# Three terms of a list scheduler's cost model changed: matmul time, a shared VectorE/GpSimd port, DRAM load latency

## The chip, the cores and the metric

The kernel runs on one core of a Trainium2 chip. The metric is the device time in microseconds of one execution. Engines are called PE (TensorE, with PEld for its weight loads), DVE (VectorE), ACT (ScalarE), POOL (GpSimd) and SP (SyncE, which issues all DMAs here).

## The reference

One layer of a hybrid encoder trunk, over 2048 rows of width 1024, all in float32. One projection `u = x @ w_in` feeds three groups of heads. Their outputs, each gated by a SiLU path, are concatenated, projected again and normalised:

```python
u = x @ w_in
(fq, fk, fv, ff, fz, mq, mk, mv, mi, mf, mo, mz, rq, rz) = jnp.split(u, split_points, axis=-1)
y_fox = forgetting_attention(fq, fk, fv, ff + fox_f_bias) * jax.nn.silu(fz)      # 6 heads x 64, causal
qk = jax.nn.silu(causal_depthwise_conv(jnp.concatenate([mq, mk], axis=-1), conv_w, conv_b))
mq_c, mk_c = jnp.split(qk, [MLSTM_WIDTH], axis=-1)
y_ml = mlstm(mq_c, mk_c, mv, mi + i_bias, mf + f_bias, mo, norm_g) * jax.nn.silu(mz)   # 4 heads x 96
mem_k, mem_v = jnp.split(mem @ w_mem_kv, [MEM_WIDTH], axis=-1)
y_mem = memory_attention(rq, mem_k, mem_v) * jax.nn.silu(rz)                     # 4 heads x 64, 256 tokens
y = jnp.concatenate([y_fox, y_ml, y_mem], axis=-1) @ w_out
return layer_norm(DEEPNORM_ALPHA * x + y, ln_g, ln_b)
```

## The kernel before

**Arithmetic.** Float32 products are made from a high and a low part of each operand in the fp32r format: three matmuls (high*high, low*high, high*low) in place of one. The parts of a loaded tile `raw` are `h` (written by ACT) and `l` (written by DVE). Attention weights come out of ACT as `ph` (high) and `p` (full), DVE makes `pl = p - ph`, and POOL sums `acc = acc + p` for the denominators.

**Tiling.** The sequence is cut into four blocks of 512 rows and two halves of two blocks each. `PROJ` lists the projection jobs: 128 columns of one head's q and k (`h`), values and gates (`v`), mLSTM rows (`r`, 288 columns) and columns (`c`), memory queries (`rq`), gates. Each job is a run of matmuls into a PSUM tile `pj`. A finished job starts the work that hangs on it.

**Attention items.** One head over one block of queries is an item; there are 40, numbered from 0 in the order in which they are added. Items 0 to 7 and 20 to 27 are memory attention (2 chunks of 128 keys each), 8 to 19 the first half of the causal heads (4 or 8 chunks), 28 to 39 the second half (12 and 16 chunks in turn). An item runs through `att_max` (maxima, tile `mx`), `att_qk` and `att_exp` (for every chunk: two matmuls into `st`, two exponentials on ACT, the subtraction `pl` on DVE, the sum `acc` on POOL), `att_pv` (for every chunk: `o<-ph,v`, then `o<-pl,v`) and `att_end`. There are two buffers for `st`, two for `p` (and one for `acc`), two for `ph` and three for `pl`, the last two with the buffers `ta` to fall back on. Items 28 to 39 run as six pairs, each pair one head's two blocks, 28 chunks.

**mLSTM and output.** When the loader has reached the output weights `wo`, `ml_unit` tiles (16 of 128 rows, two in flight) load `mq`, `mk`, `vv` and `dd` from scratch DRAM, update the state `cst` and write to `y_scr`. `out_tile` (16 tiles) reads `y_scr` as `yr`, splits it into `yh` and `ylo`, and multiplies by `wo`. The 32 buffers of the tag `x`, which hold the parts of the input, take the parts of `wo` as the last projections give them up.

**What sets the order.** Nothing of the order is written by hand beyond `PROJ`. Every piece above is a generator that yields instructions. `Machine.run` simulates the five engines while the program is built: at each step it takes the engine whose next ready instruction could start earliest by the model, and on that engine the thread of highest priority (`PRIO`: loads first, then ends and maxima, `pv`, `qk`, mLSTM, projections, output). `Op.__init__` gives an instruction's cost in ns, `Machine.when` the time at which its inputs are there (with 200 ns between engines), and `Machine.issue` advances the clocks and emits it. The order so found is the program's order on each engine; on the chip each engine runs its instructions in that order and waits on semaphores. All instructions are emitted in `issue`, so all carry one line in the profile, L204 (L212 in the changed kernel); groups are told apart by tile names.

Of the kernel before, what the change touches and what calls it, by code (L numbers as in the profile page):

```python
# [14 lines left out]
BF16 = mybir.dt.bfloat16  # L15
# [4 lines left out]
DRAM = bass.MemoryType.DRAM  # L20
# [56 lines left out]
class Op:  # L77


    def __init__(self, eng, fn, args, kw):  # L80
        self.eng, self.fn, self.args, self.kw = eng, fn, args, kw
        ap = [a for a in args if hasattr(a, "tensor")]
        out = kw.get("out", ap[0] if ap else None)
        ins = ap[1:] if "out" not in kw else ap
        ins = ins + [v for k, v in kw.items() if k != "out" and hasattr(v, "tensor")]
        self.out = out.tensor.name
        self.ins = [a.tensor.name for a in ins]
        size = lambda a: math.prod(a.shape[1:])
        cols = size(out)
        wide = max([cols] + [size(a) for a in ins])  # L90
        if eng == "PE":
            f32 = ins[0].dtype == F32
            if f32 and fn.__name__ != "transpose":
                self.cost = 2.0 * max(2.0 * cols / 2.4, 107.0)
            else:
                self.cost = max((2.0 if f32 else 1.0) * cols / 2.4, 53.0 if ins[0].dtype == BF16 else 107.0)
        elif eng == "ACT":
            self.cost = 70.0 + 0.835 * wide + 115.0 * sum(hasattr(kw.get(a), "tensor") for a in ("bias", "scale"))
        elif eng == "DVE":
            one = fn.__name__ in ("tensor_scalar", "tensor_copy")  # L100
            columns = sum(size(a) == 1 for a in ins)
            self.cost = 69.0 + (0.521 if one else 1.042) * wide + 60.0 * columns
        elif eng == "POOL":
            if kw.get("op") == ALU.pow:
                self.cost = 290.0 + 170.0 * cols
            else:
                self.cost = 120.0 + (2.15 if fn.__name__ == "tensor_tensor" else 0.95) * wide
        else:
            self.cost = 475.0
            self.nbytes = 4 * math.prod(out.shape)  # L110


class Alloc:
# [14 lines left out]
DMA_NS, DMA_BPNS = (600.0, 750.0), 366.0  # L128


class Machine:
# [5 lines left out]
    def __init__(self, make):  # L137
        self.make = make
        self.clk = dict(PE=0.0, ACT=0.0, DVE=0.0, POOL=0.0, SP=0.0)
        self.dma_clk = 0.0  # L140
        self.wr, self.rd = {}, {}
        self.slots, self.tag_of = {}, {}
        self.waiting, self.ready = [], {e: [] for e in self.clk}
        self.seq = 0
# [48 lines left out]

    def issue(self, op):
        start = max(self.clk[op.eng], self.when(op))
        end = start + op.cost
        self.clk[op.eng] = end
        if op.eng == "SP":
            self.dma_clk = max(self.dma_clk, end + DMA_NS[0]) + op.nbytes / DMA_BPNS
            end = self.dma_clk + DMA_NS[1]  # L200
        for nm in op.ins:
            self.rd[nm] = max(self.rd.get(nm, 0.0), end)
        self.wr[op.out] = (end, op.eng)
        op.fn(*op.args, **op.kw)  # L204
# [1182 lines left out]
```

## Time and profile before

| | |
|---|---|
| median of 3 runs | 1445.92 us (1445.73 to 1448.08) |
| the profiled execution's own time | 1446.53 us |
| its span | 1444.8 us |
| DVE busy | 1058.8 us (73%) |
| ACT busy | 673.1 us (47%) |
| POOL busy | 435.0 us (30%) |
| DMA, mean over the span | 105 GB/s |
| granted TensorE clock, mean | 0.987 |

A matmul's recorded duration holds its way through the array, so neighbours overlap: a 512-column matmul is recorded as about 0.40 us, but the next one starts 0.23 us after it. PE's busy share is therefore no measure of how much of its time is used; the distance from start to start is. Rows of the timeline give the start, the duration, the engine, the operation, the tiles `out<-in`, and in brackets the idle time ahead and what ended it.

### The profile page before, as it was taken

What the parts mean: (1) busy time and instruction counts of PE and PEld (TensorE: products, weight loads), DVE (VectorE), ACT (ScalarE), POOL (GpSimd) and SP (SyncE); (2) the same over time, 40 slices, a digit from 0 to 9 for tenths busy, and PEclk for the clock granted to TensorE, in tenths of its full rate; (3) what the DMA queues carried; (4) which work ended last, traced back from release to release, by engine and by line L of the source; (5) the groups of instructions that cost most, each with busy time, mean ns of one, the idle gap of its engine ahead of it and who ended that gap; (6) DMA issues with size and microseconds to landing.
All of it is one profiled execution on the core that took longest, in us unless ns stands there. A gap on an engine that the chain in (4) does not pass through costs nothing.

```text
span 1444.8 us, 22963 instructions
## 1 busy us (share of the span) xinstructions
PE 1355.7 (94%) x7904; PEld 1160.5 (80%) x7904; DVE 1058.8 (73%) x2158; ACT 673.1 (47%) x1463; POOL 435.0 (30%) x401
## 2 busy tenths in 40 slices
PE   6999999999999999999999989999998969989998
PEld 6888998998877798977787768787686757877886
DVE  5887356637588979579797788779889786767455
ACT  5444234424355643344646364544636566555100
POOL 2011002303043201013737071722726314445300
PEclk9999999999999999999999999999999979999999
DMA  6613232231322452431011402131111586765432
GB/s 200 205 46 103 79 109 86 78 115 56 116 74 74 143 177 61 131 105 54 21 49 53 121 9 61 38 104 56 58 40 56 165 239 200 216 185 160 134 134 92
DMA packets 123556, 151.81 MB, mean 105 GB/s; under 512 B 16832, under 2 KB 72080, under 8 KB 123440
## 3 DMA queue, kind: packets, MB, share of 16 engines
q1 hardware_dynamic: 123440, 150.35, 34.9%
q8 instruction: 63, 1.03, 0.3%
q14 instruction: 53, 0.43, 0.1%
HBM read 97.62 MB, written 44.00 MB: 98 GB/s over the span
## 4 chain that ended last, share of the span: by engine, by line
PE 56%; DVE 19%; POOL 6%; ACT 6%; issue 4%; DMA 3%; SPq 0%; DVEq 0%; POOLq 0%; ACTq 0%
PE pj L204 44%; POOL acc L204 6%; PE mx L204 5%; DVE pl L204 5%; PE st L204 4%; PE o L204 3%; DVE cv L204 2%; DVE mp L204 1%; ACT p L204 1%; DVE l L204 1%; DMA raw<-in_wo_dram 1%; DVE sc L204 1%; DVE y L204 1%; DVE mx L204 1%; DMA raw<-in_wg_dram 1%
## 5 line engine op out<-in xcount | busy, mean ns | idle before, releaser
L204 POOL TENSOR_TENSOR acc<-acc,p 128x512 f32<-128x512 f32 (+2 forms) x232 | 326.0, 1405 | 611.4 <-PE mx L204 223.1
L204 PE MATMUL pj<-h,h 128*128 128x288 f32 (+3 forms) x1496 | 488.5, 327 | 14.8 <-ACT h L204 8.0
L204 PE MATMUL pj<-l,h 128*128 128x288 f32 (+3 forms) x1496 | 480.4, 321 | 0.9 <-DVE l L204 0.9
L204 PE MATMUL pj<-h,l 128*128 128x288 f32 (+3 forms) x1496 | 479.3, 320 | 0.3 <-DVE l L204 0.2
L204 PEld LDWEIGHTS pj<-h,h 128*128 128x128 f32 x1496 | 284.1, 190 | 34.2 <-ACT h L204 8.2
L204 PEld LDWEIGHTS pj<-l,h 128*128 128x128 f32 x1496 | 284.3, 190 | 25.1 <-DVE l L204 2.2
L204 PEld LDWEIGHTS pj<-h,l 128*128 128x128 f32 x1496 | 283.5, 189 | 19.5 <-DVE l L204 0.7
L204 DVE TENSOR_TENSOR pl<-p,ph 128x512 fp32r<-128x512 f32 (+2 forms) x191 | 196.7, 1034 | 27.5 <-ACT p L204 20.8
L204 DVE TENSOR_TENSOR l<-raw,h 128x512 fp32r<-128x512 f32 (+2 forms) x174 | 123.1, 728 | 61.8 <-ACT h L204 58.0
L204 ACT ACTIVATE p<-st 128x512 f32<-128x512 f32 (+2 forms) x232 | 126.9, 547 | 65.7 <-POOL acc L204 32.2
L204 ACT CAST h<-raw 128x512 fp32r<-128x512 f32 (+2 forms) x174 | 107.4, 632 | 98.6 <-DMA raw<-in_wg_dram 67.8
L204 ACT ACTIVATE ph<-st 128x512 fp32r<-128x512 f32 (+2 forms) x231 | 127.7, 554 | 51.3 <-PE st L204 47.7
L204 PE MATMUL o<-pl,v 128*128 128x512 f32 (+2 forms) x268 | 110.6, 414 | 31.7 <-DVE pl L204 29.3
L204 PE MATMUL st<-qb,kb 128*128 128x512 f32 (+2 forms) x272 | 110.0, 404 | 0.0
L204 DVE TENSOR_REDUCE mp<-mx 128x1 f32<-128x512 f32 x144 | 95.1, 684 | 19.2 <-PE mx L204 18.4
L204 PE MATMUL pj<-h,yh 128*128 128x512 f32 (+1 forms) x264 | 106.6, 404 | 0.3 <-DVE dd L204 0.2
L204 PE MATMUL mx<-km,qm 66*128 66x512 f32 (+2 forms) x304 | 97.4, 359 | 6.9 <-DVE mp L204 2.8
L204 PE MATMUL st<-qm,km 68*128 68x512 f32 (+2 forms) x272 | 103.1, 379 | 0.9 <-ACT p L204 0.9
L204 PE MATMUL pj<-h,ylo 128*128 128x512 f32 (+1 forms) x264 | 102.6, 389 | 0.0
L204 PE MATMUL pj<-l,yh 128*128 128x512 f32 (+1 forms) x264 | 102.4, 388 | 0.0
L204 PEld LDWEIGHTS o<-pl,v 128*128 128x128 f32 x268 | 51.0, 191 | 63.7 <-DVE pl L204 59.5
L204 PE MATMUL o<-ph,v 128*128 128x512 f32 (+2 forms) x231 | 87.5, 379 | 0.0
(180 smaller groups left out, 1910.2 us busy)
## 6 DMA issues: line engine op xcount, KB each, us to landing
raw<-in_wg_dram SPq DMA_DIRECT2D x80, 256.0 KB
raw<-in_wg_dram SPq DMA_DIRECT2D x32, 288.0 KB
raw<-in_xt_dram SPq DMA_DIRECT2D x32, 256.0 KB
yr<-y_scr SPq DMA_DIRECT2D x32, 256.0 KB
xr<-in_x_dram SPq DMA_DIRECT2D x32, 256.0 KB
out_dram<-xr SPq DMA_DIRECT2D x32, 256.0 KB
qk_scr<-cv SPq DMA_DIRECT2D x24, 256.0 KB
qb<-qm SPq DMA_DIRECT2D x40, 128.0 KB
```

What stands on the lines that cost most here:

```text
L204: op.fn(*op.args, **op.kw)
```

## The change

Three terms of the cost model are altered; kernel code, buffers, priorities and `PROJ` stay. A matmul that is not the two-pass float32 kind costs its columns over 2.4 plus 14 ns, at least 110 ns, where it cost its columns over 2.4, at least 107 (53 for bf16). A DVE or POOL instruction with more than one input in SBUF of more than one column (`op.port`) cannot start before the last such instruction of either engine has ended. A DMA whose source is in DRAM is taken to arrive 800 ns later.

```diff
+        there = [a for a in ins if a.tensor.space == "SB" and size(a) > 1]
+        self.port = len(there) > 1 if eng in ("DVE", "POOL") else False
...
-                self.cost = max((2.0 if f32 else 1.0) * cols / 2.4, 53.0 if ins[0].dtype == BF16 else 107.0)
+                self.cost = max((2.0 if f32 else 1.0) * cols / 2.4 + 14.0, 110.0)
...
+            self.far = 800.0 if kw["in_"].tensor.space == "DRAM" else 0.0
...
     def issue(self, op):
         start = max(self.clk[op.eng], self.when(op))
+        if op.port:
+            start = max(start, self.port)
         end = start + op.cost
+        if op.port:
+            self.port = end
...
-            end = self.dma_clk + DMA_NS[1]
+            end = self.dma_clk + DMA_NS[1] + op.far
```

The same instructions are emitted on every engine; their order differs, and with it which of several buffers a tile gets. Three places:

PE, inside item 29, from one chunk's low product `o<-pl` to the next chunk's. `o_8212` and `o_8215` are that item's output, `st` the next chunks' logits, `pj` a projection of mLSTM rows. Before:

```order
L204 MATMUL o_8212<-pl_8263,v_7348 128x512
L204 MATMUL o_8212<-ph_8259,v_7348 128x512
L204 MATMUL st_8280<-qm_110,km_105 128x512
L204 MATMUL st_8280<-qb_7728,kb_7643 128x512
L204 MATMUL o_8212<-pl_8279,v_7348 128x512
```

The same stretch in the changed kernel:

```order
L212 MATMUL o_8215<-pl_8275,v_7348 128x512
L212 MATMUL o_8215<-ph_8268,v_7348 128x512
L212 MATMUL pj_8288<-h_7467,h_5708 128x288
L212 MATMUL pj_8288<-l_7468,h_5708 128x288
L212 MATMUL pj_8288<-h_7467,l_5709 128x288
L212 MATMUL pj_8288<-h_7467,h_5721 128x288
L212 MATMUL pj_8288<-l_7468,h_5721 128x288
L212 MATMUL pj_8288<-h_7467,l_5722 128x288
L212 MATMUL pj_8288<-h_7470,h_5759 128x288
L212 MATMUL pj_8288<-l_7471,h_5759 128x288
L212 MATMUL pj_8288<-h_7470,l_5760 128x288
L212 MATMUL o_8215<-pl_8285,v_7348 128x512
```

Nine projection matmuls now stand between the two products, and the next logits have moved out of the stretch, ahead of it.

PE, where the first mLSTM unit begins (`mq` and `mk` are its queries and keys, `pj_12823` and `pj_12910` the third and the second projection from the last, `pj_12879` the last one, `o_12607` the output of item 39). Before:

```order
L204 MATMUL pj_12896<-mq_12824,mk_12825 128x128 x4
L204 MATMUL pj_12823<-h_5773,h_12524 128x512
L204 MATMUL pj_12823<-l_5774,h_12524 128x512
L204 MATMUL pj_12823<-h_5773,l_12525 128x512
L204 MATMUL pj_12910<-h_5979,h_12527 128x512
L204 MATMUL pj_12910<-l_5980,h_12527 128x512
L204 MATMUL pj_12910<-h_5979,l_12528 128x512
L204 MATMUL pj_12913<-ident_r,mk_12825 128x96 x4
```

In the changed kernel:

```order
L212 MATMUL pj_12963<-mq_12460,mk_12461 128x128 x4
L212 MATMUL pj_12879<-h_6115,h_12440 128x512
L212 MATMUL pj_12879<-l_6116,h_12440 128x512
L212 MATMUL pj_12879<-h_6115,l_12441 128x512
L212 MATMUL o_12607<-ph_12868,v_11063 128x384
L212 MATMUL pj_13019<-ident_r,mk_12461 128x96 x4
L212 MATMUL o_12607<-pl_12940,v_11063 128x384
L212 MATMUL pj_13026<-vv_12886,dd_12462 128x97 x4
L212 MATMUL pj_13044<-mq_12974,mk_12975 128x128 x4
```

Before, item 39 had ended and projections stand between the unit's steps; now the three last projection matmuls stand behind the unit's first step, and the end of item 39 lies among the units' steps.

SP, from the loads of mLSTM unit 1 (`mq_12915`, `mq_12974`) on. Before:

```order
L204 DMA mq_12915<-qk_scr_126 96x4x128
L204 DMA mk_12916<-qk_scr_126 96x4x128
L204 DMA vv_12918<-row_scr_131 128x388
L204 DMA dd_12917<-m_scr_150 128x4x128
L204 DMA so_12951<-row_scr_130 128x384
L204 DMA gz_12952<-row_scr_130 128x384
L204 DMA qk_scr_128<-cv_12909 128x512
L204 DMA mq_12984<-qk_scr_126 96x4x128
```

In the changed kernel:

```order
L212 DMA mq_12974<-qk_scr_126 96x4x128
L212 DMA mk_12975<-qk_scr_126 96x4x128
L212 DMA vv_12977<-row_scr_131 128x388
L212 DMA dd_12976<-m_scr_150 128x4x128
L212 DMA qk_scr_129<-cv_12916 128x512
L212 DMA raw_12992<-in_wo_dram 128x512
L212 DMA raw_12997<-in_wo_dram 128x512
L212 DMA qk_scr_128<-cv_12878 128x512
L212 DMA raw_13005<-in_wo_dram 128x512
L212 DMA raw_13011<-in_wo_dram 128x512
L212 DMA raw_13050<-in_wo_dram 128x512
```

Loads of `wo` now follow unit 1's loads directly, and 12 of them stand between the first load of unit 0 and the first load of unit 2, where none stood.

More of the change, by code (lines that the diff above doesn't have):

```diff
@@ L139, in __init__ @@
         self.clk = dict(PE=0.0, ACT=0.0, DVE=0.0, POOL=0.0, SP=0.0)
-        self.dma_clk = 0.0
+        self.dma_clk = self.port = 0.0
         self.wr, self.rd = {}, {}
```

## The prediction

> **What bounds the kernel now.** First the page: how much of the span each engine is busy, and the chain that ended last.
>
> ```profile
> span 1444.8 us, 22963 instructions
> PE 56%; DVE 19%; POOL 6%; ACT 6%; issue 4%; DMA 3%; SPq 0%; DVEq 0%; POOLq 0%; ACTq 0%
> ```
>
> PE holds most of the chain; the other engines hold over a third of it. So PE's work is the floor, and what an order can win or lose is the time in which PE waits for something that came too late. The views of who waited for whom say for what. The first row is of the whole span, the other two of 668.7 to 1127.5 us alone, in which the causal items of the second half run (columns: in all, times, longest).
>
> ```profile
> PEld o L204 <- DVE pl L204: 59.5, 94, 2.2
> ...
> PEld o L204 <- DVE pl L204: 48.5, 75, 2.2
> ...
> PE o L204 <- DVE pl L204: 24.2, 38, 2.0
> ```
>
> PE's costliest wait is the low part `pl` of a chunk's weights, and 48.5 of its 59.5 us fall into that stretch. PE's own row is smaller, since a recorded matmul is longer than the distance to the next. One such wait, and the distances, in the timeline of PE inside item 29:
>
> ```profile
> 693.66 0.39 PE L204 MATMUL o<-pl,v 128*128 128x512 f32 x1
> 693.88 0.29 PE L204 MATMUL pj<-h,h 128*128 128x288 f32 x1
> 694.01 0.29 PE L204 MATMUL pj<-l,h 128*128 128x288 f32 x1
> 694.15 0.30 PE L204 MATMUL pj<-h,l 128*128 128x288 f32 x1
> 694.28 0.40 PE L204 MATMUL st<-qm,km 68*128 68x512 f32 x1
> 694.52 0.40 PE L204 MATMUL st<-qb,kb 128*128 128x512 f32 x1
> 694.75 0.40 PE L204 MATMUL o<-ph,v 128*128 128x512 f32 x1
> ...
> 695.25 0.29 PE L204 MATMUL pj<-h,l 128*128 128x288 f32 x1
> 697.53 0.58 PE L204 MATMUL o<-pl,v 128*128 128x512 f32 x1 [1.99 <-DVE pl L204]
> ```
>
> From start to start a 288-column matmul takes 0.13 us and a 512-column one 0.23 to 0.24. Between 695.25 and 697.53 nothing else was queued that could run. Why `pl` is late shows in the groups of DVE and POOL by shape:
>
> ```profile
> L204 DVE TENSOR_TENSOR pl<-acc,ph 128x512 fp32r<-128x512 f32 x39 | 26.5, 679 | 6.7 <-ACT acc L204 6.6
> L204 DVE TENSOR_TENSOR pl<-p,ph 128x512 fp32r<-128x512 f32 x129 | 137.7, 1072 | 24.2 <-ACT p L204 18.2 <-PE pj L204 1.2 <-PE st L204 1.0
> L204 POOL TENSOR_TENSOR acc<-acc,p 128x512 f32<-128x512 f32 x160 | 255.9, 1599 | 441.0 <-PE mx L204 176.8 <-PE o L204 88.4 <-ACT p L204 86.9
> ```
>
> An item's first chunk has no sum on POOL beside it, and its `pl` takes 0.68 us; the others take 1.07 in the mean. VectorE and POOL hinder each other, and the model of before counted neither. Each pair of items in the second half is a window of its own:
>
> ```profile
> 668.70:717.70 49.00, 43.67 (x221) 33.92 (x220) 42.02 (x55) 31.61 (x65) 37.28 (x29) 0.97 0.05 14
> 741.10:789.20 48.10, 44.13 (x255) 35.99 (x254) 40.76 (x51) 31.43 (x63) 36.83 (x26) 1.00 0.14 40
> 825.00:874.20 49.20, 44.50 (x222) 34.18 (x221) 42.88 (x59) 31.52 (x65) 37.19 (x26) 0.97 0.05 15
> 898.20:947.80 49.60, 45.79 (x260) 37.88 (x260) 40.07 (x52) 31.19 (x63) 36.96 (x26) 0.97 0.12 34
> 988.20:1051.70 63.50, 57.14 (x268) 43.45 (x266) 56.40 (x79) 39.40 (x76) 37.47 (x26) 1.00 0.18 57
> 1072.90:1127.50 54.60, 48.63 (x237) 37.38 (x236) 51.40 (x69) 36.18 (x71) 37.33 (x26) 1.00 0.20 60
> 1119.50:1189.00 69.50, 54.10 (x313) 45.52 (x312) 54.81 (x132) 45.54 (x114) 18.35 (x19) 0.88 0.69 197
> ```
>
> Columns: window, length, then busy time and count of PE, PEld, DVE, ACT, POOL, granted clock, DMA share, GB/s. Four pairs with different counts of matmuls (221 to 260) have the same length, 48 to 50 us for 28 chunks. They are paced by the chain of a chunk (ACT, `pl`, `acc`, two `p` buffers) at some 1.75 us a chunk, and PE has time over in them. The seventh window is the passage from attention to output, taken up below.
>
> **Term 1, the six pairs.** No instruction is added or removed. A pair's own PE work is 120 attention matmuls (64 of `st`, 56 of `o`) and some 17 of transposes and maxima; priced from start to start, short ones less, that is 26.5 us. The rest of PE's work in a pair is projections put in as fill. In the program's order their number between a pair's first `st` and last `o` was 84, 120, 84, 123, 129 (99 of them of 512 columns) and 99 (54 of 512), and becomes 141, 126, 120, 132, 180 (114) and 171 (144). At 0.13 and 0.23 us (the 256-column ones of pairs two and four at 0.12, an estimate a little under the 288-column distance) the fill goes from 11.2, 14.4, 11.2, 14.8, 26.5 and 18.3 us to 18.8, 15.1, 16.0, 15.8, 34.7 and 36.3. Window less 26.5 less fill is PE's empty time: 11.3, 7.2, 11.5, 8.3, 10.5 and 9.8, in all 58.6 us, a little over the waits of the stretch since the half-clock matmuls after a long wait are in it. If the windows kept their length, the fill of after would leave 3.7, 6.5, 6.7, 7.3, 2.3 and 0: 26.5. So up to 32 us are to be had, and every matmul of fill is one that PE needn't do outside, where its projections run without waits.
>
> All of it would come only if fill were free. It isn't: each projection brings reads of PSUM on ACT and DVE and often a load to split. The fifth window shows it: 26.5 us of fill, and still 10.5 empty, with DVE busy 56.40 of 63.50. So the bounds are 0 and 32, and I take two thirds, **22 us**, nearer the upper end because in four of six windows POOL is idle a fourth of the time and the pace has been the same for 221 matmuls and for 260.
>
> After the wait shown above the clock is slower for a while; the next matmuls of 512 columns start 0.42 us apart, not 0.23:
>
> ```profile
> 697.91 0.63 PE L204 MATMUL o<-ph,v 128*128 128x512 f32 x1
> 698.33 0.63 PE L204 MATMUL st<-qm,km 68*128 68x512 f32 x1
> 698.76 0.63 PE L204 MATMUL st<-qb,kb 128*128 128x512 f32 x1
> ```
>
> That is the 0.97 of three windows, some 1.5 us in each, and I count it as going with the waits. [...]
>
> **Term 2, the earlier items.** 11.0 us of the waits for `pl` lie outside the stretch (59.5 less 48.5). There the order moves both ways: the causal items of the first half get a little more fill, the memory items less, as their two chunks now follow each other closely. At most 11 us could go; as much could come, if the memory items wait as the long ones do now. I take **0**, with ends at -8 and +8.
>
> **Term 3, the passage.** From the first load of the first mLSTM unit to the first matmul of the output projection:
>
> ```profile
> 1119.47 0.44 SPq L204 DMA_DIRECT2D mq<-qk_scr  x1
> ...
> 1172.01 0.39 PE L204 MATMUL pj<-h,l 128*128 128x512 f32 x1
> ...
> 1180.65 1.58 PE L204 MATMUL pj<-vw,kr 128*96 128x97 f32 x8 [3.74 <-ACT kr L204]
> ...
> 1189.00 0.77 PE L204 MATMUL pj<-h,yh 128*128 128x512 f32 x1
> ```
>
> These 69.5 us hold a chain: units 0 to 4, two in flight, the loads of `wo`, and the first `yr`. The last projection matmul starts at 1172.01, so projections cover most of it, and still PE waits, 3.74 us at once at the end. In the changed order PE has 13.6 us more work (60 matmuls of 512 columns) ahead of the first unit's first matmul, because item 39 is stretched, and once the projections are done only the end of item 39 and the units are left, each step waiting for the one before. The chain begins 13.6 us of PE work later, so if it takes as long as before it costs 13.6 us. Against that, `wo` is issued in one block right behind unit 1's loads, and 13 of its 16 loads no longer follow unit 2's. The chain is then nearer to what its bytes need: 197 GB/s over 69.5 us are 13.7 MB, and the best slice about there moved 239 GB/s:
>
> ```profile
> GB/s 200 205 46 103 79 109 86 78 115 56 116 74 74 143 177 61 131 105 54 21 49 53 121 9 61 38 104 56 58 40 56 165 239 200 216 185 160 134 134 92
> ```
>
> At that rate it is 57 us, 12 less. The term lies between +13.6 and +1; I take **+3**, near the lower end, because SP's order has the bytes queued early. Queued behind these loads on SP are the loads of units 2 and 3, and for those PE waits: that is the slower rival below. After 1189 the same output work follows in both kernels.
>
> **The sum.** The profiled execution took 1446.53 us (its span and 1.7 around it): 1446.5 - 22 + 0 + 3 = 1427.5. The median shown is 0.6 below that execution, so 1427.
>
> **The rivals.**
>
> *The fill slows the pace (0.15).* Fill brings DVE work with two SBUF inputs (splits of loads, convolution steps), which meets `acc` on POOL. For it: the fifth window, 14 us longer than the first four. Against it: the second and fourth, with a third more fill than the first at equal length. Then a quarter of the 32 us comes, 8, and with +3 the time is 1441.
>
> *The bare passage costs more than the pairs give (0.15), slower.* With no projections left, units 2 and 3 wait behind 12 loads of `wo`, 3.1 MB, at 239 GB/s 13 us, on top of the 13.6 by which the chain starts late: +27 less a gain of 8 to 22 gives +5 to +19, about 1457. It decides from the point where the chain from the first unit's load to the first output matmul takes over 78 us (69.5 and the 22 - 13.6 left). For it: the 3.74 us wait of unit 3, and the granted clock of 0.88 in that window. Against it: those loads have to be made anyway before the output projection can start.
>
> *The change doesn't do what it says (0.06).* If `pl` and `acc` keep their places relative to each other and what PE gains in the pairs it waits for elsewhere, by `mx` or PSUM buffers, nothing shows: 1446. Against it: the counts of fill above.
>
> *All of the empty time goes (0.10).* 32 us from the pairs, a passage of 57 us, and some of term 2: 1446.5 - 32 - 5 = 1410 or a little less.
>
> **How the numbers follow.** The forecast, 1415 to 1438, has 0.54. A measurement of this kernel can't tell less than 0.2% (2.9 us) from no change. Faster: 0.54, 0.10, and 0.12 of the first rival's 0.15, in all 0.76. Same: 0.06 and 0.03 of that rival, 0.09. Slower: 0.15. The range reaches from 1407, below the best case, to 1447, past the first and third rival, and leaves out the slower one and the tails, just under 0.2.
>
> **What would show it.** Right: the wait of PEld for `pl` falls from 59.5 to about 30 us; the pairs of items 28 to 35 keep 48 to 51 us with more projection matmuls in them; the span from the first `mq` load to the first `pj<-h,yh` is 57 to 70 us. Wrong: pairs that grow by as much as their fill (first rival), a passage over 78 us with PE waiting for `cst` or `kr` of units 2 and 3 (second), or the same waits under another name, such as `mx` behind `mp` or `h` behind loads. An error in term 1 weighs most.

## The result, and the profile after

| | before | after |
|---|---|---|
| median | 1445.83 us (1444.22 to 1448.08, 4 runs) | 1468.15 us (1464.93 to 1471.69, 4 runs) |
| the profiled execution, its span | 1446.53, 1444.8 us | 1469.72, 1468.0 us |
| mean granted TensorE clock | 0.987 | 0.963 |

The changed kernel is slower: the ratio is 1.0154, with a 95% interval of 1.0125 to 1.0183. Ratios, here and below, leave out the few executions that ran far slower at a lower clock; medians are over all. The prediction, 1427 and at most 1447, was wrong in sign. From the page after, the span and the chain by engine:

```profile
span 1468.0 us, 22935 instructions
PE 63%; DVE 19%; issue 5%; DMA 5%; ACT 5%; POOL 2%; SPq 1%; DVEq 0%; POOLq 0%; ACTq 0%
```

PE's share of the chain rose from 56 to 63%, as one would wish, and the span rose with it. The waits over the whole span, of after and then two of before that the prediction did not show (in all, times, longest):

```profile
ACT ph L212 <- PE st L212: 98.3, 85, 4.8
PEld o L212 <- DVE pl L212: 49.2, 58, 3.4
ACT p L212 <- POOL acc L212: 11.8, 26, 1.1
```

```profile
ACT ph L204 <- PE st L204: 47.7, 69, 3.2
...
ACT p L204 <- POOL acc L204: 32.2, 64, 1.0
```

The wait for `pl` fell from 59.5 to 49.2 us, not to 30. In its place ScalarE waits twice as long for `st`, that is for PE: before, POOL's `acc` held the chunks back (32.2 us), now the scores come late. The windows of the six pairs, columns as in the prediction, and the passage from the first `mq` load (1152.39) to the first `pj<-h,yh` (1224.29):

```profile
681.40:735.40 54.00, 48.93 (x280) 40.65 (x279) 46.19 (x61) 33.14 (x71) 36.93 (x32) 1.00 0.09 24
757.30:813.10 55.80, 48.83 (x264) 39.44 (x262) 45.84 (x56) 32.54 (x65) 36.21 (x26) 0.88 0.15 45
847.20:898.00 50.80, 46.97 (x258) 37.52 (x256) 44.51 (x63) 32.27 (x69) 37.10 (x26) 1.00 0.07 18
919.60:975.20 55.60, 48.05 (x269) 39.38 (x267) 46.45 (x56) 32.06 (x65) 36.25 (x26) 0.93 0.14 44
1013.10:1085.00 71.90, 68.25 (x320) 54.44 (x319) 56.87 (x86) 39.87 (x79) 38.57 (x26) 0.95 0.18 58
1104.50:1195.90 91.40, 80.70 (x379) 66.23 (x377) 79.64 (x132) 58.59 (x125) 41.29 (x30) 0.87 0.43 127
...
1152.40:1224.30 71.90, 58.77 (x299) 51.86 (x297) 56.18 (x140) 49.31 (x129) 26.72 (x26) 0.69 0.71 207
```

Every pair is longer: by 5.0, 7.7, 1.6, 6.0, 8.4 and 36.8 us. The fill did go in (280 matmuls for 221 in the first), but the windows did not keep their length. From the end of the last pair to the first `pj<-h,yh` it is 28.4 us (1195.9 to 1224.3) where it was 61.5 (1127.5 to 1189.0): the passage now begins well inside pair 38.

How much of that is loss? For each stage, take PE's work as the sum of the distances that its matmuls have from start to start when nothing waits (0.12, 0.13 and 0.23 us for 256, 288 and 512 columns); what the stage takes beyond it is lost. Worked out from the starts of all matmuls in both traces, us:

| stage | lost before | lost after | difference | forecast |
|---|---|---|---|---|
| up to the first item | 17.9 | 28.2 | +10.3 | none made |
| items 0 to 27 | 25.2 | 31.7 | +6.5 | 0 (-8 to +8) |
| the six pairs | 61.1 | 77.1 | +16.0 | -22 (-32 to 0) |
| between the pairs | 5.7 | 12.9 | +7.2 | none made |
| behind the last pair | 34.1 | 17.3 | -16.8 | +3 (+1 to +13.6) |
| sum | 144.0 | 167.2 | +23.2 | -19 |

The sum is the difference of the spans; slightly different prices and borders move a stage's difference by up to 2.4 us. Pair by pair:

| pair | lost before, after | fill added, us | `l` and `cv` before, after |
|---|---|---|---|
| 28 | 11.7, 8.6 | 8.0 | 0, 2 |
| 30 | 8.0, 14.5 | 1.2 | 0, 4 |
| 32 | 11.8, 8.5 | 5.0 | 0, 0 |
| 34 | 8.8, 13.8 | 1.1 | 0, 4 |
| 36 | 10.7, 10.6 | 8.4 | 18, 21 |
| 38 | 10.1, 21.1 | 25.9 | 11, 43 |

`l` splits a load, `cv` is a step of the convolution; both are VectorE operations with two inputs in SBUF. Of the 25.9 us added to pair 38, 18.0 are projections; the rest are 72 matmuls of the first two mLSTM units, which the prediction's count of fill left out. Where much fill and two or none of the `l` and `cv` came in (28, 32), the loss did fall. Where more of them came in (30, 34, 38), it rose; in pair 36, with three more, it did not.

### The profile page after: what moved, and what is told of

Its sections match the earlier page's. It is cut to its first block, busy times and chain, and to the rows that moved or that the text cites. A ratio compares the mean times of both kernels' runs of the same rounds, so it can differ in the third digit from the quotient of the medians.

```text
span 1468.0 us, 22935 instructions
## 1 busy us (share of the span) xinstructions
PE 1377.9 (94%) x7904; PEld 1185.0 (81%) x7904; DVE 1058.9 (72%) x2158; ACT 666.6 (45%) x1463; POOL 430.5 (29%) x401
## 4 chain that ended last, share of the span: by engine, by line
PE 63%; DVE 19%; issue 5%; DMA 5%; ACT 5%; POOL 2%; SPq 1%; DVEq 0%; POOLq 0%; ACTq 0%
PE pj L212 47%; PE st L212 6%; PE o L212 5%; PE mx L212 5%; DVE pl L212 4%; DVE cv L212 2%; DVE l L212 2%; DVE mp L212 2%; POOL acc L212 2%; DVE y L212 1%; ACT h L212 1%; SPq L212 1%; DMA raw<-in_xt_dram 1%; DVE mx L212 1%; DMA raw<-in_wg_dram 1%
## 5 line engine op out<-in xcount | busy, mean ns | idle before, releaser
L212 POOL TENSOR_TENSOR acc<-acc,p 128x512 f32<-128x512 f32 (+2 forms) x232 | 322.4, 1389 | 660.7 <-ACT p L212 247.4
L212 PE MATMUL pj<-h,h 128*128 128x288 f32 (+3 forms) x1496 | 492.1, 329 | 13.2 <-ACT h L212 10.7
L212 PEld LDWEIGHTS pj<-h,h 128*128 128x128 f32 x1496 | 287.5, 192 | 34.4 <-ACT h L212 11.3
L212 PEld LDWEIGHTS pj<-l,h 128*128 128x128 f32 x1496 | 287.6, 192 | 29.9 <-DVE l L212 6.0
L212 PEld LDWEIGHTS pj<-h,l 128*128 128x128 f32 x1496 | 286.7, 192 | 19.8 <-DVE l L212 0.9
L212 DVE TENSOR_TENSOR pl<-p,ph 128x512 fp32r<-128x512 f32 (+2 forms) x180 | 173.3, 973 | 31.6 <-ACT p L212 28.2
L212 ACT ACTIVATE ph<-st 128x512 fp32r<-128x512 f32 (+2 forms) x218 | 120.4, 558 | 112.4 <-PE st L212 98.3
L212 DVE TENSOR_TENSOR l<-raw,h 128x512 fp32r<-128x512 f32 (+2 forms) x174 | 129.3, 761 | 51.2 <-ACT h L212 50.3
L212 DVE TENSOR_REDUCE mp<-mx 128x1 f32<-128x512 f32 x144 | 94.8, 683 | 11.8 <-PE mx L212 11.2
L212 PEld LDWEIGHTS o<-pl,v 128*128 128x128 f32 x272 | 53.4, 197 | 54.1 <-DVE pl L212 49.2
```

## The experiments

**Each term alone.** Each kernel is the kernel before with one of the three terms; the diffs are the hunks of the change for that term.

```diff
m_only:
+                self.cost = max((2.0 if f32 else 1.0) * cols / 2.4 + 14.0, 110.0)
p_only:
+        self.port = len(there) > 1 if eng in ("DVE", "POOL") else False
f_only:
+            self.far = 800.0 if kw["in_"].tensor.space == "DRAM" else 0.0
```

> Only the matmul term of the change. If the port term makes the slow order: 1443-1449, as before. If any reordering of this size costs: 1455-1475, with the half-clock time above 70 us.

> Only the port term. If the port term makes the slow order: 1462-1475. If it is a better model spoilt by the other two terms: 1420-1440. If any reordering of this size costs: 1455-1475, no different from the other two terms alone.

> Only the 800 ns on loads from DRAM. If the port term makes the slow order: 1443-1449. If any reordering of this size costs: 1455-1475.

Measured: 1496.1 us (ratio 1.0358, 1.0342 to 1.0375), 1480.21 (1.0247, 1.0218 to 1.0277) and 1459.33 (1.0103, 1.0086 to 1.012). All three are slower alone, by 51, 35 and 14 us, and together by 22: the terms don't add, and the first two lie above every range that was expected. Only the port term clearly lengthens the pairs (53.8 and 60.5 us for the first two; 48.5 and 49.8 with the matmul term, 48.1 and 47.8 with the loads'). The matmul term loses in the items 0 to 27, 53.7 us for 25.2.

**The clock.** The clock fell from 0.987 to 0.963. Is that cause or symptom? The changed order, with the 65 places at which PE waits 0.5 us or more filled by matmuls with zero weights:

```diff
+            for _ in range(WARM.get(self.pe, 0)):
+                op.fn(out[:, 0:P], self.zero, self.ident, start=op.kw["start"], stop=op.kw["start"])
```

> The changed kernel, same order on every engine; at 65 places where its trace shows PE waiting 0.5 us or more, PE gets matmuls with an all-zero stationary tile (0.115 us each, for 85% of the wait) ahead of the waiting one, adding zero to its output. Clock theory (the waits are as long in sum as before, 138 against 142 us, but lie so that the clock is halved for 110 us instead of 39): time half-clock falls below 40 us and the time to 1440-1450. Rival (the waits themselves are the loss, the clock only marks them): 1465-1472, whatever the clock does.

Measured: 1466.02 us, clock 0.981. The time at half clock fell from 110 to 59 us, and the kernel gained 2 us, within the spread. Its windows stay as long (55.6, 54.8, 50.7 and 55.9 us for the first four), and ScalarE still waits 99.1 us for `st`. So the clock accounts for little of the loss. The half clock did not go below the 40 us expected; the 59 us that stayed (39 in the kernel before) this run does not price.

**VectorE's operations in a pair.** Into the kernel before, at the same sixteen places in the windows 28 to 34 (four in each, behind a `pl`), goes an addition on VectorE with two inputs, a maximum on VectorE with one, or a copy on ScalarE:

```diff
+            if self.dve - 1 in ADD:
+                self.nc.vector.tensor_tensor(self.scr, self.mrow, self.mrow, op=ALU.add)   # add_tt
+                self.nc.vector.reduce_max(self.scr[:, 0:1], self.mrow, axis=AX.X)           # add_red
+                self.nc.scalar.copy(self.scr, self.mrow)                                    # add_act
```

> The kernel before with sixteen additions of 512 columns of VectorE put in, each with two inputs in SBUF and a result that nothing reads, four behind certain `pl` operations in each window of the pairs 28, 30, 32 and 34. Split theory: each costs a turn of 1.7 us, so each of the four windows grows by 6 to 8 us from 48 to 49 us and the time by 20 to 27, to 1466 to 1473. Rival (VectorE has room between its `pl` operations, 28 of 0.7 to 1.1 us in 48 us, so it takes these beside the rest): 1446 to 1451.

> The control of the run with sixteen additions: at the same sixteen places a maximum over 512 columns of VectorE, one input in SBUF, some 0.7 us each. Split theory: there is room for it beside POOL's `acc`, 0 to 5 us in all, 1446 to 1451. Rival (any added operation of VectorE delays the chunks that stand behind it): sixteen times 0.7, 11 us, 1455 to 1459.

> The kernel before with sixteen copies of 512 columns on ScalarE, at the sixteen places where the additions on VectorE cost 21 us and the maxima nothing. ScalarE makes the high part `h` of each load with such an operation, some 0.6 us. If ScalarE has room in a chunk (it is busy 35 of 49 us in these windows): 0 to 4 us, 1445 to 1450. If the high parts delay the chunk as well: 0.6 us each and more, 10 to 20 us, 1455 to 1466.

Measured: 1466.83 us (ratio 1.0139, 1.0109 to 1.0168), 1444.75 (0.9998, 0.9979 to 1.0017) and 1448.3 (1.0018, 1.0006 to 1.0031). The four windows with the additions:

```profile
666.60:720.40 53.80, 45.85 (x221) 35.64 (x220) 47.19 (x59) 30.84 (x65) 36.95 (x29) 0.90 0.05 13
743.80:798.90 55.10, 47.05 (x255) 38.47 (x254) 45.59 (x55) 30.50 (x63) 36.92 (x26) 0.94 0.11 35
834.30:888.90 54.60, 48.03 (x221) 37.85 (x220) 49.88 (x63) 31.06 (x65) 36.47 (x26) 0.87 0.05 13
913.10:967.40 54.30, 46.01 (x259) 37.76 (x258) 46.15 (x56) 30.38 (x63) 36.87 (x26) 0.97 0.13 37
```

They grew by 4.8, 7.0, 5.4 and 4.7 us, 21.9 for sixteen operations, 1.4 us each. An operation with one input costs nothing at the same places, one on ScalarE 0.2 us. The maxima are recorded as 0.67 us each, the additions, with POOL's `acc` beside them, as 1.77. So it is not room on VectorE that is short (the maxima found it) but its turns against POOL's `acc`. In the trace after, the same is seen in pair 30 (VectorE, POOL and PE):

```profile
792.27 8.45 POOL L212 TENSOR_TENSOR acc<-acc,p 128x512 f32<-128x512 f32 x5
...
796.06 3.53 DVE L212 TENSOR_TENSOR l<-raw,h 128x512 fp32r<-128x512 f32 x2
...
801.32 0.80 PE L212 MATMUL o<-pl,v 128*128 128x512 f32 x1 [2.39 <-DVE pl L212]
...
802.34 0.63 PE L212 MATMUL o<-pl,v 128*128 128x512 f32 x1
```

Two splits take 3.53 us between two `pl`; beside POOL they take 1.77 each. PE then waits 2.39 us and goes on at half clock: the next 512-column matmuls start 0.43 us apart, not 0.23. The ends of the `pl` about there, in us from the window's start, are 37.2, 38.9, then 44.0: two turns of 1.7 are lost at once, and two more between 45.4 and 50.6.

**The splits and loads taken out of the changed order.** In split_out the low parts of ten loads in the windows 28, 30 and 34 are zeros; in load_out the ten loads are left out whole; in p38_out the 43 operations of pair 38 are fills with zeros. In place of each operation taken out stands a fill of 0.5 us on VectorE.

```diff
+            if self.dve - 1 in NARROW:
+                self.nc.vector.memset(op.args[0].bitcast(F32), 0.0)
+                return
```

> The changed kernel with its order, but ten of VectorE's `l<-raw,h` (the low parts of loads, each 1.7 to 1.8 us with two inputs in SBUF) that stand in the windows of the pairs 28, 30 and 34 replaced by a fill with zeros, which reads nothing: the low parts of those loads are left out of the computation. Split theory (each such operation costs the chunk chain of a pair a whole turn of `acc`, about 1.7 us): the windows of the changed kernel, 54.0, 55.8 and 55.6 us, shrink by 2, 4 and 4 turns, to about 51, 49 and 49 us, and the time from 1468 to 1450 to 1458. Rival (the length is set by what TensorE has to do in the windows, or by the order of its instructions): windows within 1 us of before, time 1464 to 1471.

> The changed kernel in its order, with the ten loads whose low parts stand in the windows 28, 30 and 34 left out whole: no transfer, no `h` on ScalarE, no `l` on VectorE; both parts are filled with zeros, so ten blocks of weights are left out of the computation. Leaving out the low parts alone gave 6.5 us. Load theory (a load in a pair costs by its `l`, by its `h` in ScalarE's queue, and by the wait of that `h` for the transfer): windows 30 and 34 go from 55.8 and 55.6 to 48 to 51 us, window 28 from 54.0 to 51 to 53, and the time to 1450 to 1457. Rival (the rest of the growth is due to the fill's place and order): windows as without the low parts, 55, 52 and 54, time 1459 to 1465.

> The changed kernel in its order, with the 43 operations of VectorE in the window of pair 38 that split loads (`l`, 19) or make steps of the convolution (`cv`, 24) replaced by a fill with zeros, which reads nothing: those low parts and those steps are left out of the computation. The window lost 21.1 us in the changed kernel and 10.1 in the kernel before, where 17 such operations stand. If they take the chunk chain's turns: the window falls from 91.4 to 75 to 83 and the time to 1450 to 1460. If the fill moved into it (26 us more of PE's work) sets its length: 89 to 92, time 1464 to 1470.

Measured: 1461.68 us (1.0105, 1.0076 to 1.0134), 1465.66 (1.0149, 1.0134 to 1.0164) and 1462.17 (1.0112, 1.009 to 1.0131). Window 30 without the low parts, and window 38 without its 43 operations:

```profile
755.80:807.50 51.70, 46.45 (x264) 38.29 (x262) 40.33 (x56) 32.24 (x65) 36.15 (x26) 0.96 0.16 49
```

```profile
1103.10:1188.10 85.00, 77.36 (x379) 64.06 (x377) 62.33 (x132) 58.56 (x125) 40.74 (x30) 0.94 0.46 136
```

Window 30 gives back 4.1 of the 7.7 us, and in it the `pl` end at 39.7, 41.4, 43.1 and 44.8, without the two stops. Window 38 gives back 6.4 us of its 11.0 of loss (11 such operations stood in it before, not the 17 that the expectation names); its 85.0 us lie between the 75 to 83 and the 89 to 92 that were expected. But window 34 gives back only 1.2 and window 28 gets 1.1 longer. What the removal gives is thus far less than what the addition costs: some 0.4 us an operation in the first three windows and 0.15 in window 38, against 1.4. The theory holds for the two stops of window 30 and fails in the windows 28 and 34. Load_out is a poor test, since its twenty fills of 0.5 us stand on VectorE at the same places and made stops of their own there (3.0 us from `pl` to `pl` where split_out has 1.7).

**The fill itself.** Fill_even and fill_lump put 280 zero-weight matmuls (128 columns, counted at 0.115 us each, an estimate a little above the 0.11 from start to start of such matmuls in the trace before; 32 us) into the kernel before, in the windows 28 to 34; fill_out takes 150 projection matmuls, 19.0 us, out of the same windows of the changed order.

```diff
+            for _ in range(FILL.get(self.pe, 0)):
+                op.fn(op.args[0][:, 0:P], self.zero, self.ident, start=op.kw["start"], stop=op.kw["start"])
...
+            if self.pe - 1 in OUT and not (op.kw["start"] or op.kw["stop"]):
+                return
```

> The kernel before, its order untouched, with fill that does nothing: in the four windows of the pairs 28 to 34 a matmul of 128 columns with zero weights (0.115 us each) ahead of each of the 56 `o` matmuls, two ahead of every fourth, 70 in a window, 8.0 us, about what the first of these windows gains in the changed kernel. No VectorE, ScalarE or DMA work comes with it. Forecast's view (PE's 8 to 12 empty us in each window take fill and the length stays): windows 48 to 50 us, time 1445 to 1450. Loop theory (matmuls that stand in PE's queue between a chunk's `st` and its `o` delay the chunk behind, since PE waits for `pl`, VectorE for `p`, and ScalarE for `st` in turn): each window grows by 4 to 8 us, time 1461 to 1478.

> The kernel before with the same 280 matmuls of zero weights as in the run with even fill, 8.0 us in each of the windows 28 to 34, but in lumps of ten (1.15 us) ahead of every eighth `o`. Spread evenly they cost 6.7 us in all, and the four windows grew by 4.8 of the 32 us put in. Lump theory (what lengthens the windows of the changed kernel is that its fill stands in runs of 0.75 us and more, 14, 6, 11 and 7 of them against 4 in each window before): the windows grow by 4 us and more each, 1460 to 1475. Rival (PE's own fill is nearly free however it is dealt, and the loads that come with it cost): 1449 to 1456.

> The changed kernel in its order, with 150 projection matmuls (the middle one of a group of three, `pj<-l,h`) of the windows 28, 30, 32 and 34 left out of the computation: 5.5, 4.3, 4.7 and 4.6 us of PE's work, 19.0 in all; everything else, the reads of PSUM and the loads too, stays. In the real order the four windows grew by 20.2 us for 15.3 us of fill. If the fill lengthens them one for one: 54.0, 55.8, 50.8 and 55.6 become 48 to 51 each, and the time 1446 to 1453. If the chain of the chunks in its new order sets the length, and PE only fills what is there: windows within 1.5 us of before, time 1462 to 1468.

Measured: 1452.25 us (1.0048, 1.0026 to 1.007), 1452.85 (1.0046, 1.0028 to 1.0064) and 1460.83 (1.0108, 1.0087 to 1.0129). Windows with even fill, then windows with the fill taken out:

```profile
668.00:717.40 49.40, 47.52 (x292) 41.14 (x290) 42.25 (x55) 31.91 (x65) 37.59 (x30) 1.00 0.05 15
741.60:792.30 50.70, 49.18 (x325) 43.81 (x324) 39.33 (x53) 31.24 (x63) 37.42 (x26) 1.00 0.13 38
...
902.20:953.80 51.60, 49.81 (x330) 44.33 (x328) 40.53 (x55) 30.80 (x63) 37.44 (x26) 1.00 0.15 41
```

```profile
678.30:732.40 54.10, 47.57 (x239) 36.80 (x237) 46.63 (x61) 32.87 (x71) 36.68 (x32) 0.97 0.08 23
754.30:808.90 54.60, 47.19 (x228) 36.55 (x226) 45.87 (x56) 32.24 (x65) 36.05 (x26) 0.86 0.15 46
...
915.60:969.60 54.00, 46.27 (x232) 35.61 (x230) 46.98 (x56) 31.98 (x65) 36.25 (x26) 0.89 0.15 45
```

In the old order 32 us more on PE lengthen the four windows by 4.9 us, and lumps do no more harm than even fill. In the new order 19 us less shorten them by 3.6. Both ways a microsecond of PE's fill is worth 0.15 to 0.2. So in these windows PE's own time in the fill really is nearly free, as the prediction had it, and it is not what makes them longer. What comes with a projection, its reads of PSUM on ScalarE and VectorE, fill_out leaves in place; by add_act and add_red an operation with one input costs 0.2 us or nothing, but no run takes these reads out. Window 28, which grew by 5.0 us, is 54.1 us without 5.5 us of its fill and 55.1 without its two low parts: neither explains it.

**Up to the first item.** After loses 10.3 us more than before ahead of item 0. VectorE's order there has small gate operations ahead of splits: for one of them it waits 4.16 us, until 35.78, with two splits behind it, and a chain of them runs from 49.25 to 54.05, ahead of the split that PE waits 3.41 us for. Three of PE's waits there, the first of them ahead of both:

```profile
29.16 0.59 PE L212 MATMUL pj<-h,h 128*128 128x270 f32 x1 [2.36 <-ACT h L212]
51.15 0.39 PE L212 MATMUL pj<-h,h 128*128 128x256 f32 x1 [0.90 <-ACT h L212]
54.95 0.58 PE L212 MATMUL pj<-l,h 128*128 128x256 f32 x1 [3.41 <-DVE l L212]
```

Late_start applies the three terms only from the model's 62nd microsecond:

```diff
+        LATE[0] = self.clk["PE"] > 62000.0
...
+        if op.port and LATE[0]:
```

> The changed kernel with its three terms in force only from the model's 62nd microsecond, so that the order up to the first item is that of the kernel before and the pairs hold the same counts of fill as in the changed kernel (141, 126, 120, 132, 180, 171). Theory that 10 us of the 23 lost are lost before the first item: that stretch goes back from 88.0 to 74 to 76 us and the time is 1454 to 1461. Rival (the start's loss is only shifted work and comes back behind it): 1464 to 1470.

Measured: 1463.49 us (1.0128, 1.0101 to 1.0155). The loss up to the first item falls from 28.2 to 16.8, and the time by 4.7 us only: some 5 us come back in later stages (items 1.2, pairs 2.3, the rest 2.0). Both sides of the expectation were too sharp; about half of the start's loss is real.

**The plan's pace.** By the model's own clocks a pair of 28 chunks takes 37 us before and 50 to 52 after: a full chunk costs 1.22 us there for `acc` alone, and 1.82 once `pl` and `acc` take turns. Port_soft holds the port 120 ns less for VectorE; late28b has that port alone, and only while the pairs are ordered.

```diff
+            self.port = end - (120.0 if op.eng == "DVE" else 0.0)
...
+        if op.port and 580000.0 < self.clk["PE"] < 955000.0:
```

> The changed kernel with the common port held 120 ns less by an operation of VectorE, so that a chunk's `pl` and `acc` take 1.70 us in the model in place of 1.82, which is the pace measured. The counts of fill become 129, 156, 108, 153, 165, 162, and the model's windows 49 to 50 us, the last 59.6 in place of 87.0. Theory that the lost time comes from fill dealt out for a pace that is too slow: the windows are 50 to 53 us, the last about 62, and 6 to 12 us of the 23 come back: 1456 to 1462. Rival (any fill of this amount delays the loop, at whatever pace it was planned): windows 52 to 58, time 1463 to 1475.

> A version meant to keep what the port term gives and leave the rest: the kernel before with the common port alone, held 120 ns less by VectorE, and in force only while the pairs from item 28 on are ordered. Fill of the six windows 17.6, 10.8, 17.6, 10.4, 36.4 and 23.2 us (before 11.2, 14.4, 11.2, 14.8, 26.5, 18.2), splits of loads 0, 4, 0, 4, 6, 3 (before 0, 0, 0, 0, 6, 6). Theory that more fill in a window costs little and each split 1.4 us: windows 28 and 32 stay at 49 to 51 with 6 us more fill each, a gain of 3 to 5 us each, windows 30 and 34 grow to 51 to 54 with 4 us less fill, a loss of 6 to 9 us each, and the sum is a little slower than before: 1446 to 1456. Rival (fill is what costs): windows 28 and 32 grow to 54 to 56, 30 and 34 stay at 47 to 49.

Measured: 1460.73 us (1.0109, 1.0085 to 1.0133) and 1473.67 (1.0205, 1.019 to 1.0221). With the softer port the pairs lose 50.6 us, 10 less than in the kernel before, though PE does 18.6 us more work in the first four windows: a gain of the kind that the prediction meant exists, 10 us of the 22. It is given back: behind the last pair 36.0 are lost (before 34.1, after 17.3), up to the first item 25.2 (17.9 before), between the pairs 15.7 (5.7), and in the items 0 to 27 some 5 more. Late28b, meant to keep the gain alone, came out 18 us above the range expected: it lost in the pairs (66.1; windows of 52 to 54 us, with or without splits) and behind them (53.8 for 34.1).

The changed model lets neither VectorE nor GpSimd start an operation with two inputs in SBUF before the other's has ended. The traces show that one holds the other up; that it does so for its whole length is not shown. In p_only a `pl` that starts first is as short as alone (0.69 us), and the `acc` that starts 0.11 us behind it ends 1.14 us after it, 1.72 us long:

```profile
784.72 0.69 DVE L212 TENSOR_TENSOR pl<-p,ph 128x512 fp32r<-128x512 f32 x1 [1.70 <-ACT p L212]
...
784.83 1.72 POOL L212 TENSOR_TENSOR acc<-acc,p 128x512 f32<-128x512 f32 x1 [0.67 <-ACT p L212]
```

At the usual pace (kernel before, 704 to 711 us) an `acc` ends 1.15 us after a `pl`, and the next `pl` 0.55 us after that, 1.70 together. Alone the two are recorded as 0.68 us and at least 1.27, so recorded lengths overstate what the pair needs, and the model's 1.82 us is 0.12 too long.

**Other orders.** The latency between engines, 200 ns, is set to 220 and to 190; none of the three terms is in these.

```diff
-LAT = 200.0
+LAT = 220.0
```

> The kernel before with one number of the model changed that has nothing to do with the three of the change: the latency between engines 220 ns in place of 200. It moves about as many of TensorE's instructions (1555 are no more in the old sequence) as the loads' 800 ns alone did, which cost 14 us. Theory that the order before is a lucky one among near orders, and that any reordering of this size loses it: 1455 to 1500. Rival (the three terms lose because of what they say, and an order made from another latency is as good): 1438 to 1451.

> The kernel before with the latency between engines 190 ns in place of 200 in the model: a second order near the old one, with 1134 of TensorE's instructions out of the old sequence. If the order before is a lucky one and neighbours cost 1 to 2%, as with 220 ns: 1456 to 1475. If 220 ns was an unlucky draw: 1440 to 1451.

Measured: 1472.5 us (1.018, 1.0154 to 1.0207) and 1459.85 (1.0109, 1.0077 to 1.0142). Both are slower, by 27 and 14 us where the change lost 22, and at other places: in the profiled executions (1464.9 and 1459.35 us) their pairs lose what they lost before (61.4 and 60.9 us), the stages behind the last pair 45.6 and 44.8 for 34.1. So an order can lose 1 to 2% for a reason that has nothing to do with the three terms. Nine reorderings ran (the change, its terms alone, late_start, port_soft, late28b, and these two), and none beat the kernel before; no experiment shows a version that would.

## Why the prediction was wrong

- **Bound, and PE's own price for fill: right.** In the pairs 28 and 32, with two splits and none come in, losses fell by 3.1 and 3.3 us (forecast two thirds of 7.6 and 4.8), and fill_even and fill_out put the price of PE's time at a fifth of its length. Yet the two windows grew by 5.0 and 1.6 us, for 8.0 and 5.0 of fill.
- **Term 1 failed, at the words "If the windows kept their length".** It was +16.0 instead of -22. The four windows of equal length, 221 to 260 matmuls, showed that PE's fill does not set the length, and that was right; I took it to mean that the new order would leave the pace alone. But the new order also moves what VectorE does: 10 splits into three windows that had none, 32 operations more into the last. An operation of this kind costs 1.4 us in the old order (add_tt), and taking them out gives back 4.1 us in window 30, 1.2 in 34 and 6.4 in 38.
- **The first rival was the right mechanism at the wrong size.** It priced these operations at three quarters of a gain of 32 us, so it still ended faster, at 1441. Counting them (10 and 32) and giving each the 1.7 us of an `acc` turn, 71 us, would have put the pairs on the slower side, though further than they went: removal shows that most of them cost less.
- **What is left of term 1 is open.** Of the 22.5 us that the pairs 30, 34 and 38 lost more, removal gave back about 12. The rest, and longer windows without any split (28 and 32 are 53.8 and 51.7 us in p_only, 52.1 each in late28b), may lie in the order of the chunks' own instructions: ScalarE waits for `st` where it waited for `acc`. No run isolates that. The placing of fill within a pair is a candidate, since in the changed order pair 30 has all of it ahead of its last nine chunks; but in late28b it ends earlier still, 25 us into that pair, and the window is shorter, 52.2 us.
- **Term 2** was +6.5 with an end at +8. **Nothing was forecast for the start**, which lost 10.3, about half of it for good, **nor between the pairs**, +7.2.
- **Term 3** went the other way, and by an overlap that it left out: the passage took 71.9 us and did not get shorter (57 to 70 were forecast), but 43.5 us of it now lie inside pair 38, where 8.0 did, and the stages behind that pair lost 16.8 us less. The loads of `wo` with their splits had moved into pair 38 (DMA share 0.43 for 0.20), so part of that pair's 11 us may be the price of this gain. Port_soft shows the trade: pair 38 back to 6.1 us of loss, the stages behind it to 36.0. The second rival, a passage of over 78 us, did not happen.
- **The half clock** was rightly taken as a companion of the waits: 51 us less of it are worth 2 us (warm_after).

The larger error is one of kind. The prediction carried a gain in one stage to the end and took other stages as unmoved. In nine reorderings stages gained up to 17 us and lost up to 39 (the pairs of p_only, an estimate by the same prices), and the kernel before is the best of the ten.

## What to carry to other kernels

A truer cost model in a list scheduler does not by itself make a faster kernel. The order is a draw, and here nine of nine neighbours of the draw in hand were slower, by 1.0 to 3.6%. So a forecast for a reordering should start at a loss of a per cent and ask for more than an argument about one stage. Count what the reordering moves on every engine, not on the busiest: an operation that competes with the pacing pair of engines can cost most of a turn of theirs (1.4 of 1.7 us in add_tt). Putting sixteen of them into the old order prices such an operation in one run, but take the price as an upper one: it was 1.4 us there, and 0.15 to 0.4 us came back where such operations were taken out of the new order.

## What was not expected of the hardware

**A busy PE that stays at half clock.** In pair 30 of p_only the clock was halved from 770.9 to 805.0 us without a break (0.75 in the mean of 740.9 to 801.4). Six equal periods without fill run in it from 777.56 to 791.92; one of them in PE's timeline:

```profile
784.74 0.79 PE L212 MATMUL st<-qm,km 68*128 68x512 f32 x1 [0.32 <-ACT p L212]
785.33 0.63 PE L212 MATMUL st<-qb,kb 128*128 128x512 f32 x1
785.76 0.63 PE L212 MATMUL o<-ph,v 128*128 128x512 f32 x1
786.18 0.63 PE L212 MATMUL o<-pl,v 128*128 128x512 f32 x1
787.13 0.79 PE L212 MATMUL st<-qm,km 68*128 68x512 f32 x1 [0.32 <-ACT p L212]
```

A period is 2.39 us; four matmuls of 0.43 us, the distance at half clock, fill 72% of it. In pair 34 of late28b, also without fill, the clock is full from 945.0 us on (0.94 in the mean of 907.4 to 961.5):

```profile
950.06 0.50 PE L210 MATMUL o<-pl,v 128*128 128x512 f32 x1 [0.49 <-DVE pl L210]
950.39 0.40 PE L210 MATMUL o<-ph,v 128*128 128x512 f32 x1
950.63 0.40 PE L210 MATMUL st<-qm,km 68*128 68x512 f32 x1
950.87 0.39 PE L210 MATMUL st<-qb,kb 128*128 128x512 f32 x1
951.75 0.50 PE L210 MATMUL o<-pl,v 128*128 128x512 f32 x1 [0.49 <-DVE pl L210]
```

Here the same four, at 0.23 us, fill 54% of a period of 1.70 us, and the clock stays full. So the busier PE stayed slow and the less busy one fast, and the slow one paid 0.69 us a chunk. At 72% busy, with 0.67 us idle a period, the full clock did not come back in 14.4 us. In the trace after, where the clock is 0.50 from 52.6 to 59.3 us, matmuls ran without a wait from 54.95 on, those of 256 columns 0.21 us apart, and from 59.37 on, 4.4 us later, they were 0.12 us apart, at full clock.

**Two inputs against one.** Sixteen VectorE operations with one input in SBUF, 0.67 us each, cost nothing (add_red, 1444.75 us); sixteen with two inputs, recorded as 1.77 us each beside POOL, cost 22 us (add_tt, 1466.83).
